# Moving the loads of an SSM's B and C, and the rows of B, between two DMA queues of a hybrid decoder block

## The chip, the cores and the metric

One core of a Trainium2 chip runs the whole block in one launch. The metric is the device time of that launch in microseconds (us), lower is better. The kernel before takes 1404.6 us (median of three runs, 1403.13 to 1407.8).

## What is computed

One residual block on x, 256 tokens by 2048 channels, in float32 (the batch and the depth are 1). Cut to what matters here:

```python
u = rms_norm(x, norm_mix_pre)
q, k, v, s_in, g_a, g_s = split(u @ w_in)          # 2048 x 8192
y_a = diff_attention(q, k, v, ...)                 # 8 heads, two softmax maps each
# S5: 64 groups of 16 channels, each drives one 64-state complex diagonal SSM
a_bar = exp(lam * dt)
b_bar = ((a_bar - 1) / lam)[..., None] * b         # (64, 64, 16), complex
bu = einsum('gph,lgh->lgp', b_bar, s_in)           # complex
states = scan(a_bar, bu)                           # over the 256 tokens
y_s = einsum('ghp,lgp->lgh', c, states).real + d * s_in
y_s = gelu(y_s); y_s = y_s * sigmoid(y_s @ w_glu + b_glu)
h = x + rms_norm((sigmoid(g_a)*(y_a@Wa) + sigmoid(g_s)*(y_s@Ws)) @ w_out)
out = h + rms_norm((silu(z@Wg) * (z@Wu)) @ Wd),  z = rms_norm(h)
```

## The kernel before, in words

**The main stream.** Nearly all of the time is a chain of dense products that TensorE does in blocks (`run_block`, line 254): one block is 256 tokens by 1024 columns, and goes through its rows of weights in steps k of 128. Each weight tile of 128x1024 (512 KB) is loaded by SyncE's queue into one of four buffers `raw` (line 186), then split in two: ScalarE rounds it (`hi`, line 205), VectorE subtracts (`lo`, line 206). Three products (hi by hi, lo by hi, hi by lo) of 512 columns for two token halves and two column halves are 12 matmuls for each k. `ensure` (line 210) keeps the splits up to two steps ahead and asks for loads up to four tiles beyond that. The first block makes the SSM's input, so it is called `ssm` and reads `w_in` from column 3072; then come q, k, v, the gates and so on.

**The start.** x is loaded in column pieces by SyncE's queue among the first weight tiles (`load_x0`, `load_x`, `first_load`, lines 340 to 347 and 972 to 980). TensorE transposes x piece by piece in the midst of the first block (`x_piece`, line 387; the tiles are `b` in the trace).

**Side tasks.** Everything else is Python generators that `pump` (line 230) advances after each step by a budget. `prep` (line 478) makes the SSM's constants: it loads the small parameters, B (`braw`, line 488) and C (`cn`, line 491) by GpSimd's queue; forms a_bar, sines and cosines on VectorE; multiplies B (`bb`); builds the rotation tables on GpSimd (lines 592 to 597); copies B's groups into block form (`blkB`, lines 617 and 618, ScalarE), transposes them, splits the result into `bh` and `bl` (tile `ga` in the trace), and writes it to DRAM as `stack_b` with twelve DMAs of 256 KB on SyncE's queue (line 627). `u_parts` (line 653) does the same for the SSM's input (`stack_u`, line 674). `ssm` (line 677) reads them back for each half group (`fetch`, line 706: `usf` and `bsf`, cast by ScalarE into `us` and `bs`), multiplies them (`bu_mm`), and rotates, scans and rotates back on VectorE, sixteen half groups in all. `table(hh)` (line 631, GpSimd) makes the rotation table of a half group's upper half, and `mirror` (line 649, ScalarE) fills the lower half from it.

**What sets the order.** Each engine and each queue works in one fixed order. The splits, matmuls and evacuations of the main stream are pinned to the order of the code (`InOrder`, line 31); side tasks on VectorE, ScalarE and TensorE, all of GpSimd's work and all DMA issues are not: a scheduler at build time places them by its own estimates of when each is ready, and among those that are ready takes the one that comes first in the code (line 1432). An instruction that has to wait on the chip holds up everything behind it on its engine or queue.

Of the kernel before, what the change touches and what calls it, by code (L numbers as in the profile page):

```python
# [88 lines left out]
def hybrid_block_kernel(  # L89
# [7 lines left out]
    nc = tc.nc  # L97
    pin = [True]
    V, A, T = (InOrder(tc, e, pin) for e in (nc.vector, nc.scalar, nc.tensor))
    G = nc.gpsimd  # L100
# [377 lines left out]
    def prep():  # L478
# [6 lines left out]
        braw = [big8(shape=(32, 2048)) for _ in range(2)]  # L485
        for ap, r, n in rows:
            G.dma_start(prow[r:r + n, :], ap)
        for t_, ap in zip(braw, (ssm_b_re, ssm_b_im)):
            G.dma_start(t_, ap[0].rearrange("(a g) p h -> a (g p h)", g=2))
        cn = [mixp.tile([P, NG, 64], F32, name=nm("cn")) for _ in range(2)]  # L490
        for t_, ap in zip(cn, (ssm_c_re, ssm_c_im)):
            G.dma_start(t_, ap[0].rearrange("(a g) h p -> (g h) a p", g=8))
        ldt = pp.tile([32, 2], F32, name="ldt")
        G.dma_start(ldt, ssm_log_dt[0].rearrange("(a g) -> a g", g=2))
        lamv = pp.tile([P, 4, 64], F32, name="lamv")
# [17 lines left out]
        e1 = pp.tile([P, 34], F32, name="e1")  # L513
        dve_exp(e1, e_in, 34, pp)
        yield 2.0

        nlam = const.tile([P, 1], F32, name="nlam")
        V.tensor_tensor(nlam, e1[:, 33:34], e1[:, 32:33], op=ALU.subtract)
# [8 lines left out]
        dve_exp(rr, adt, 32, pp)  # L527
        hold["rr"] = rr
        yield 2.0
        th = pp.tile([P, 8, 32], F32, name="th")  # L530
        V.tensor_tensor(th[:, 0, :], aim, dt, op=ALU.mult)
        for l in range(1, 8):
# [78 lines left out]
        for gg in range(NG // 2):  # L611
            ps = side()
            for e in range(2):
                g = 2 * gg + e
                for o in range(2):
                    t_ = blkB[e][o]
                    A.copy(t_[0:64, :, 0:16], bb[o][0:64, 4 * g:4 * g + 4, :])
                    A.copy(t_[64:128, :, 16:32], bb[o][64:128, 4 * g:4 * g + 4, :])
                    transpose(ps[:, (2 * e + o) * P:(2 * e + o + 1) * P], t_.rearrange("p a b -> p (a b)"))
            gs = slice(2 * gg, 2 * gg + 2)  # L620
            src = ps.rearrange("p (a o q) -> p a o q", a=2, o=2)
            A.copy(bh[:, gs].bitcast(F32R), src)
            V.tensor_tensor(bl[:, gs], src, bh[:, gs], op=ALU.subtract)
            yield 0.7
        for n, t_ in enumerate((bh, bh, bl)):
            for j in range(4):
                nc.sync.dma_start(stack_b[:, j // 2, n, :, j % 2].rearrange("g q o n -> q g o n"), t_[32 * j:32 * j + 32])  # L627
                yield 0.2


    def table(hh):
# [21 lines left out]
    def u_parts():  # L653

        un = hold["u"]
        uT = big8(shape=(P, 8, S))
        hold["yT"] = uT
        uh, ul = big8(shape=(P, 8, S)), big8(shape=(P, 8, S))
        for kk in range(4):
            ps = side()  # L660
            for j in range(2):
                for t in range(2):
                    k = 2 * kk + j
                    transpose(ps[:, j * S + t * P:j * S + t * P + P],
                              un[:, t * 1024 + k * P:t * 1024 + (k + 1) * P])
            ks = slice(2 * kk, 2 * kk + 2)
            fl = lambda t_: t_[:, ks, :].rearrange("p a b -> p (a b)")
            A.copy(fl(uT), ps)
            A.copy(fl(uh).bitcast(F32R), ps)
            V.tensor_tensor(fl(ul), ps, fl(uh), op=ALU.subtract)  # L670
            yield 0.6
        for n, t_ in enumerate((uh, ul, uh)):
            for j in range(4):
                nc.sync.dma_start(stack_u[:, j // 2, n, :, j % 2].rearrange("g q n -> q g n"), t_[32 * j:32 * j + 32])
                yield 0.3

    def ssm():
        uT = hold["yT"]
        nxt = table(0)
        mirror(*nxt)  # L680

        def finish(g, bC, sre, sim):
            yp = side()
# [44 lines left out]
        yield from group(0)  # L728
        fetch(0)
        bu = bu_mm(0)  # L730
        fetch(1)
        yield 1.0
        for hh in range(2 * NG):
# [703 lines left out]
```

## Time and profile before

| what | value |
|---|---|
| runs | 1407.8, 1403.13, 1404.6 us; median 1404.6 us |
| profiled execution | 1409.3 us, of which the span of the trace is 1407.5 us |
| TensorE (PE) | 1367.2 us busy, 97% of the span |
| VectorE (DVE) | 885.9 us, 63% |
| ScalarE (ACT) | 688.7 us, 49% |
| GpSimd (POOL) | 167.3 us, 12% |
| SyncE's DMA queue (q1) | 260.09 MB |
| GpSimd's DMA queue (q0) | 1.30 MB |

The span is the time from the first to the last recorded instruction; 1.8 us lie around it. Busy time of matmuls is modelled (they are pipelined), so the number of matmuls in a stretch and the clock that TensorE was granted tell more of its pace than its busy share. A row of the timeline gives start and length in us, engine, line, operation, destination and sources, and in brackets how long the engine sat idle before it and what ended that. L41 is the line of the helper that records all pinned engines' instructions, so there the tile's name tells what it is. SPq, ACTq and POOLq are the DMA issues of SyncE, ScalarE and GpSimd.

### The profile page before, as it was taken

The numbers are of one execution on the slowest core, as the hardware profiler recorded it, in microseconds if no ns is written. First come the engines' busy times: TensorE is split into PE (matmuls) and PEld (weight loads), VectorE is DVE, ScalarE is ACT, GpSimd is POOL, SyncE is SP. The second block draws the span as 40 slices with busy tenths as digits, with TensorE's granted clock in tenths as the row PEclk, the third lists the DMA queues.
The fourth block names the chain that finished last, engine by engine and source line by source line (L and its number), as shares of the span: only waits on it lengthen the run. The fifth ranks groups of instructions, "written<-read, shape, count | busy, mean of one in ns | idle before, by whom it ended". The sixth has DMA issues, their size and how long they took to land.

```text
span 1407.5 us, 17397 instructions
## 1 busy us (share of the span) xinstructions
PE 1367.2 (97%) x6367; PEld 1114.8 (79%) x6367; DVE 885.9 (63%) x1124; ACT 688.7 (49%) x1019; POOL 167.3 (12%) x187
## 2 busy tenths in 40 slices
PE   7999999999999989999999999999999999999997
PEld 6877777777777778888888888888888888888885
DVE  4954999768999957655754444444444445555555
ACT  3646545687544455444554434444444444444443
POOL 3090344202334100000000000000000000000001
PEclk8999999999999999999999999999999999999999
DMA  8678765454565657655765565655656555565551
GB/s 246 195 231 251 214 191 177 146 150 143 178 186 171 180 168 261 189 174 195 248 216 191 168 211 178 198 180 191 201 179 199 169 198 202 179 211 174 203 179 60
DMA packets 102006, 266.70 MB, mean 189 GB/s; under 512 B 10176, under 2 KB 17168, under 8 KB 98528
## 3 DMA queue, kind: packets, MB, share of 16 engines
q1 hardware_dynamic: 100704, 260.09, 57.6%
q10 hardware_dynamic: 608, 4.20, 0.8%
q0 software_dynamic: 608, 1.30, 0.4%
q8 instruction: 50, 0.82, 0.2%
q14 instruction: 36, 0.29, 0.1%
HBM read 257.16 MB, written 8.39 MB: 189 GB/s over the span
## 4 chain that ended last, share of the span: by engine, by line
issue 53%; PE 29%; DVE 9%; POOL 3%; ACT 3%; DMA 2%; SPq 1%; POOLq 0%; DVEq 0%; ACTq 0%
PE acc L41 26%; DVE lo L41 2%; PE side L41 2%; ACT hi L41 1%; DVE ssB L41 1%; DVE ssA L41 1%; DVE ssD L41 1%; DVE ssC L41 1%; DMA b<-in_x_dram 1%; SPq L627 1%; ACT b L41 1%; POOL tabS L644 1%; DVE ga L41 0%; DVE sim L41 0%; ACT prob L41 0%
## 5 line engine op out<-in xcount | busy, mean ns | idle before, releaser
L41 DVE TENSOR_TENSOR lo<-raw,hi 128x1024 fp32r<-128x1024 f32 (+1 forms) x341 | 422.6, 1242 | 256.2 <-ACT hi L41 246.5
L41 ACT CAST hi<-raw 128x1024 fp32r<-128x1024 f32 (+1 forms) x340 | 355.3, 1051 | 344.4 <-PE acc L41 278.8
L41 PE MATMUL acc<-lo,zT_h 128*128 128x512 f32 x704 | 275.1, 391 | 0.0
L41 PE MATMUL acc<-hi,zT_l 128*128 128x512 f32 x704 | 274.3, 390 | 0.0
L41 PE MATMUL acc<-hi,zT_h 128*128 128x512 f32 x704 | 271.2, 393 | 0.2 <-ACT zT_h L41 0.2
L41 DVE TENSOR_TENSOR lo<-b,hi 128x1024 fp32r<-128x1024 f32 x124 | 151.1, 1224 | 147.4 <-ACT hi L41 147.4
L41 PE MATMUL acc<-lo,xT_h 128*128 128x512 f32 x512 | 204.6, 403 | 2.6 <-DVE lo L41 2.4
L41 PE MATMUL acc<-hi,xT_l 128*128 128x512 f32 x512 | 202.0, 398 | 0.0
L41 ACT CAST hi<-b 128x1024 fp32r<-128x1024 f32 x124 | 130.6, 1053 | 120.4 <-PE acc L41 104.0
L41 PE MATMUL acc<-hi,xT_h 128*128 128x512 f32 x512 | 162.6, 403 | 5.2 <-ACT hi L41 3.1
L41 PEld LDWEIGHTS acc<-hi,zT_h 128*128 128x128 f32 x704 | 132.3, 188 | 27.6 <-ACT zT_h L41 0.7
L41 PEld LDWEIGHTS acc<-hi,zT_l 128*128 128x128 f32 x704 | 132.3, 188 | 27.6
L41 PEld LDWEIGHTS acc<-lo,zT_h 128*128 128x128 f32 x704 | 132.3, 188 | 26.5
L41 PEld LDWEIGHTS acc<-lo,xT_h 128*128 128x128 f32 x512 | 98.2, 192 | 27.4 <-DVE lo L41 4.9
L41 PEld LDWEIGHTS acc<-hi,xT_h 128*128 128x128 f32 x512 | 96.3, 191 | 27.9 <-ACT hi L41 5.6
L41 PEld LDWEIGHTS acc<-hi,xT_l 128*128 128x128 f32 x512 | 98.1, 192 | 19.8 <-issue 0.4
L41 PE MATMUL acc<-hi,b 128*128 128x512 f32 x256 | 82.9, 399 | 0.4 <-DVE b L41 0.3
L398 POOL TENSOR_TENSOR rstdf<-rstdfm,half 128x1 f32<-128x1 f32 x2 | 1.1, 546 | 691.6 <-DVE rstdfm L41 691.6
L41 PE MATMUL acc<-lo,hTh 128*128 128x512 f32 x176 | 68.6, 390 | 0.0
L41 PE MATMUL side<-hi,hTh 128*128 128x512 f32 x176 | 68.5, 389 | 0.0
L41 PE MATMUL side<-lo,hTh 128*128 128x512 f32 x176 | 68.5, 389 | 0.0
L41 PE MATMUL acc<-hi,hTh 128*128 128x512 f32 x176 | 68.4, 391 | 0.0
(213 smaller groups left out, 1699.2 us busy)
## 6 DMA issues: line engine op xcount, KB each, us to landing
raw<-in_w_in_dram SPq DMA_DIRECT2D x127, 512.0 KB, 4.1
raw<-in_w_ffn_gate_dram SPq DMA_DIRECT2D x96, 256.0 KB, 2.8
raw<-in_w_ffn_up_dram SPq DMA_DIRECT2D x96, 256.0 KB, 3.1
raw<-in_w_ffn_down_dram SPq DMA_DIRECT2D x44, 512.0 KB, 3.7
b<-in_w_ffn_down_dram SPq DMA_DIRECT2D x22, 1024.0 KB, 4.9
b<-in_w_ffn_gate_dram SPq DMA_DIRECT2D x40, 512.0 KB, 3.8
b<-in_w_ffn_up_dram SPq DMA_DIRECT2D x40, 512.0 KB, 4.7
raw<-in_w_out_dram SPq DMA_DIRECT2D x32, 512.0 KB, 4.4
```

Of the source, the lines that this page charges most:

```text
L41: ins = f(*a, **kw)
L398: G.tensor_tensor(r, ms, half[:, :n], op=ALU.pow)
L627: nc.sync.dma_start(stack_b[:, j // 2, n, :, j % 2].rearrange("g q o n -> q g o n"), t_[32 * j:32 * j + 32])
L644: G.tensor_tensor(up(tss), hi(sa), lo(cb), op=ALU.mult)
```

## The change

The bulk loads of B and C leave GpSimd's queue at the start of `prep` and go to SyncE's, B after the first exponential of `prep` and C after the second. Of each pair of copies into `blkB` the second goes from ScalarE to VectorE. The twelve writes of `stack_b` go from SyncE's queue to GpSimd's, with the six rows of first half groups ahead of the six of second half groups; those of `stack_u` take the same order and stay on SyncE's queue. The mirror of the first table stands after the first fetch and product in the code.

```diff
@@ prep
         braw = [big8(shape=(32, 2048)) for _ in range(2)]
         for ap, r, n in rows:
             G.dma_start(prow[r:r + n, :], ap)
-        for t_, ap in zip(braw, (ssm_b_re, ssm_b_im)):
-            G.dma_start(t_, ap[0].rearrange("(a g) p h -> a (g p h)", g=2))
         cn = [mixp.tile([P, NG, 64], F32, name=nm("cn")) for _ in range(2)]
-        for t_, ap in zip(cn, (ssm_c_re, ssm_c_im)):
-            G.dma_start(t_, ap[0].rearrange("(a g) h p -> (g h) a p", g=8))
...
         dve_exp(e1, e_in, 34, pp)
         yield 2.0
+        for t_, ap in zip(braw, (ssm_b_re, ssm_b_im)):
+            nc.sync.dma_start(t_, ap[0].rearrange("(a g) p h -> a (g p h)", g=2))
...
         dve_exp(rr, adt, 32, pp)
         hold["rr"] = rr
         yield 2.0
+        for t_, ap in zip(cn, (ssm_c_re, ssm_c_im)):
+            nc.sync.dma_start(t_, ap[0].rearrange("(a g) h p -> (g h) a p", g=8))
...
                     A.copy(t_[0:64, :, 0:16], bb[o][0:64, 4 * g:4 * g + 4, :])
-                    A.copy(t_[64:128, :, 16:32], bb[o][64:128, 4 * g:4 * g + 4, :])
+                    V.tensor_copy(t_[64:128, :, 16:32], bb[o][64:128, 4 * g:4 * g + 4, :])
...
-        for n, t_ in enumerate((bh, bh, bl)):
-            for j in range(4):
-                nc.sync.dma_start(stack_b[:, j // 2, n, :, j % 2].rearrange("g q o n -> q g o n"), t_[32 * j:32 * j + 32])
-                yield 0.2
+        for hf in range(2):
+            for n, t_ in enumerate((bh, bh, bl)):
+                for j in (2 * hf, 2 * hf + 1):
+                    G.dma_start(stack_b[:, hf, n, :, j % 2].rearrange("g q o n -> q g o n"), t_[32 * j:32 * j + 32])
+                yield 0.1
@@ u_parts
-        for n, t_ in enumerate((uh, ul, uh)):
-            for j in range(4):
-                nc.sync.dma_start(stack_u[:, j // 2, n, :, j % 2].rearrange("g q n -> q g n"), t_[32 * j:32 * j + 32])
-                yield 0.3
+        for hf in range(2):
+            for n, t_ in enumerate((uh, ul, uh)):
+                for j in (2 * hf, 2 * hf + 1):
+                    nc.sync.dma_start(stack_u[:, hf, n, :, j % 2].rearrange("g q n -> q g n"), t_[32 * j:32 * j + 32])
+                    yield 0.3
@@ ssm
         nxt = table(0)
-        mirror(*nxt)
...
         yield from group(0)
         fetch(0)
         bu = bu_mm(0)
+        mirror(*nxt)
         fetch(1)
```

## Rows read from the trace of the kernel before

**Rows 1.** The page: busy time, share of the span and instructions by engine.
```profile
PE 1367.2 (97%) x6367; PEld 1114.8 (79%) x6367; DVE 885.9 (63%) x1124; ACT 688.7 (49%) x1019; POOL 167.3 (12%) x187
```

**Rows 2.** Windows: length, busy us (and count) of PE, PEld, DVE, ACT, POOL, clock, DMA share, GB/s.
```profile
10.00:15.00 5.00, 0.47 (x1) 0.18 (x1) 1.62 (x2) 1.42 (x2) 1.46 (x3) 0.64 1.05 224
95.00:110.00 15.00, 12.62 (x49) 9.35 (x48) 5.00 (x5) 9.77 (x27) 10.28 (x16) 0.89 0.48 152
125.00:130.00 5.00, 5.00 (x24) 4.05 (x24) 1.23 (x1) 1.32 (x2) 0.00 (x0) 1.00 0.96 246
130.00:145.00 15.00, 12.27 (x48) 9.38 (x47) 6.64 (x8) 7.67 (x13) 0.00 (x0) 0.89 0.94 301
```

**Rows 3.** Timeline of the start: TensorE's two waits, GpSimd's late issue, SyncE's weight loads.
```profile
13.56 0.47 PE L41 MATMUL side<-ident,b 128*128 128x128 f32 x1 [4.13 <-DMA b<-in_x_dram]
14.59 0.53 POOL L497 DMA_DIRECT2D ga<-in_lambda_k_dram  x1 [3.48 <-DMA b<-in_ssm_b_re_dram]
...
16.76 0.90 PE L41 MATMUL side<-ident,b 128*128 128x128 f32 x3 [2.72 <-DMA b<-in_x_dram]
16.78 22.66 SPq L308 DMA_DIRECT2D raw<-in_w_in_dram  x8
```

**Rows 4.** DMA of 0 to 30 us: totals, queues, issues with KB each and us to landing.
```profile
DMA packets 3511, 8.10 MB, mean 270 GB/s; under 512 B 606, under 2 KB 1198, under 8 KB 3446
...
q0 software_dynamic: 608, 1.30, 18.4%
...
raw<-in_w_in_dram SPq DMA_DIRECT2D x8, 512.0 KB, 8.6
...
b<-in_ssm_b_re_dram POOLq DMA_DIRECT2D x1, 256.0 KB, 9.6
...
cn<-in_ssm_c_im_dram POOLq DMA_DIRECT2D x1, 256.0 KB, 12.7
```

**Rows 5.** Timeline, 66 to 105 us: GpSimd beside VectorE, then ScalarE and TensorE at the first table.
```profile
70.75 0.31 POOL L592 TENSOR_TENSOR sre<-tabc,ga 128x64 f32<-128x64 f32 x1
...
71.03 1.39 DVE L41 TENSOR_TENSOR lo<-raw,hi 128x1024 fp32r<-128x1024 f32 x1
...
71.41 1.22 POOL L594 TENSOR_TENSOR tabc<-sre 128x64 f32<-128x64 f32 x1
...
86.94 1.03 ACT L41 COPY blkB<-bb 64x64 f32<-64x64 f32 x4 [4.41 <-DVE bb L41]
...
99.81 0.40 ACT L41 COPY tabC<-tabC 128x256 f32<-128x256 f32 x1 [7.90 <-POOL tabC L643]
...
101.63 0.33 PE L41 MATMUL side<-ident,blkB 128*128 128x128 f32 x1 [2.17 <-ACT blkB L41]
...
104.63 0.41 ACT L41 COPY tabC<-tabC 128x256 f32<-128x256 f32 x1
```

**Rows 6.** Timeline, 117 to 155 us: SyncE's queue, then who waited, then GpSimd's next work.
```profile
117.64 11.99 SPq L627 DMA_DIRECT2D stack_b<-ga  x12
...
131.91 0.37 SPq L711 DMA_DIRECT2D bsf<-stack_b  x1
...
135.03 1.04 ACT L41 CAST hi<-raw 128x1024 fp32r<-128x1024 f32 x1 [8.70 <-DMA raw<-in_w_in_dram]
136.13 1.21 PE L41 MATMUL acc<-hi,xT_h 128*128 128x512 f32 x4 [2.68 <-ACT hi L41]
138.71 0.62 ACT L41 CAST bs<-bsf 96x512 fp32r<-96x512 f32 x1 [0.42 <-DMA bsf<-stack_b]
154.55 2.68 POOL L644 TENSOR_TENSOR tabS<-tabs,tabc 128x256 f32<-128x256 f32 x1 [48.64 <-DVE ssB L41]
```

**Rows 7.** The chain that ended last: start us, length us, what.
```profile
4.49 12.22 DMA b<-in_x_dram
...
129.73 5.21 DMA raw<-in_w_in_dram
```

**Rows 8.** DMA issues of the whole span: KB each and us to landing.
```profile
stack_b<-ga SPq DMA_DIRECT2D x12, 256.0 KB, 4.4
```

## The prediction, made before the changed kernel was run

> **What bounds the kernel now.** I read the page first: TensorE is busy for 97% of the span and no other engine for more than 63% [rows 1]. So the time is TensorE's work plus the stretches in which it falls behind, and a change that takes no matmul away can only win back such stretches. The view that finds them counts matmuls by window. An undisturbed window of 5 us has 24 at the full clock, 0.208 us each [rows 2]; three stretches in the reach of the diff have far fewer.
>
> The first is the start: one matmul from 10 to 15 us, at DMA engines that are full (share 1.05) [rows 2]. The timeline shows TensorE waiting for x twice, 4.13 and 2.72 us, until 16.76 us [rows 3], and the chain that ended last runs through that load of x for 12.22 us [rows 7]. Beside x and the weights, GpSimd's queue moves 1.30 MB and takes 18.4% of the DMA engines in the first 30 us; 1.05 MB of it are the four loads of B and C, which land 9.6 to 12.7 us after their issue [rows 4].
>
> The second is 95 to 110 us: 49 matmuls where 72 fit, so 23 x 0.208 = 4.8 us are lost [rows 2]. ScalarE stands 7.90 us before the mirror of the first table because GpSimd has not finished it, and TensorE's own wait of 2.17 us ends on ScalarE's copy into the block form of B [rows 5]. The rest of the loss is the clock: the mean granted over the window is 0.89 [rows 2], so part of it ran at the lower of TensorE's two levels, 1.2 instead of 2.4 GHz.
>
> The third is 130 to 145 us: 48 of 72, 24 x 0.208 = 5.0 us lost [rows 2]. SyncE's queue is occupied by the twelve writes of B's rows for 11.99 us, the weights come behind them, ScalarE waits 8.70 us for a tile and TensorE 2.68 us for ScalarE [rows 6]; the chain names that very load, 5.21 us [rows 7].
>
> **The change part by part.** The profiled execution took 1409.3 us, 4.7 above the median of the runs; each term below is taken off its time and the sum then carried to the median.
>
> *B and C off the start.* At the mean rate of the first 30 us, 270 GB/s, 1.05 MB take 3.9 us; by GpSimd's share of the engines (18.4% of 30 us, times 1.05/1.30) 4.5 us [rows 4]. The last of it landed after the wait for x had ended, so I take 3.5. The most that can be won is the whole wait, 4.13 + 2.72 = 6.9 us; the least is nothing, if the loads come so early on SyncE's queue that they delay the weight tiles that TensorE needs next. The four loads cost SyncE issue time: at 1.0 us each, as the writes of B's rows (11.99 / 12) [rows 6], 4 us. That is covered, since SyncE spreads eight weight issues over 22.66 us [rows 3]; without that cover the 4 us would count. GpSimd gets through its issues sooner too: the one at 14.59 us stood 3.48 us for the landing of B [rows 3]. Nobody needs it earlier.
>
> *Half of the copies into block form to VectorE.* A copy takes ScalarE 1.03 / 4 = 0.26 us [rows 5]; sixteen move, 4.1 us. Only those count that ScalarE does while it catches up after its 7.90 us: four of the copies that stand between the next splits, 1.0 us. Bounds: nothing, and the 4.1. On VectorE the copies are covered, for it is busy for 5.00 of the 15 us [rows 2]; were it full they would cost what they win.
>
> *The mirror later in the code.* I cost it at nothing. Its place in the code is not its place on ScalarE: the second table's mirror, which stands in the code after the first scans, came at 104.63 us, right behind the first's, since the scheduler took it as soon as it held it ready [rows 5]. So I expect the first to stay where GpSimd's lag is met. Bounds: 0 and the rest of the second loss, 4.8 - 1.0 = 3.8 us.
>
> *B's rows on GpSimd's queue.* SyncE gets 11.99 us back, and with them the 5.0 us lost by TensorE. GpSimd's engine can take the issues: it does nothing until 154.55 us, after an idle time of 48.64 us, and what stands behind them is only the third half group's table [rows 6]. At 0.53 us an issue [rows 3] six take 3.2 us; with a landing of 9.6 us [rows 4] the first half is there some 13 us after its rows are ready, where before the last write was issued after 11 and landed in 4.4 [rows 8]. So the readback starts no later. New is that weights and rows now share the DMA engines: at the start, beside GpSimd's queue, a weight tile landed in 8.6 us [rows 4], and four buffers at one step of 12 x 0.208 = 2.5 us each hold 10.0 us, of which the split takes 1.04 [rows 6] and some 1.39 [rows 5] and leaves 7.6. A landing of 8.6 misses that by 1.0 us, which I add. Bounds of this new wait: 0, and the whole 5.0 given back or more (the rival below).
>
> The rule against this part is in the Trainium skill's page "DMA: Bandwidth & Descriptors", section "Issuing engines are not separate DMA queues": transfers from all queues run on the same 16 engines and interleave, so another issuer only saves issue time, usually small beside the transfer. Here the issue is not small by the rows: 1.0 us each against 4.4 to land [rows 6, 8]. By the rule alone, the sum would be that of the second rival.
>
> *The order of the rows and of the input's rows* adds and removes no DMA: the same twelve writes each. The first readback needs six instead of twelve; it is counted above. What lies behind 145 us is not touched but may be scheduled in another order; I allow 2.2 us either way, the shortest of TensorE's waits on an engine above [rows 5].
>
> **Sum:** 3.5 + 1.0 + 5.0 - 1.0 = 8.5 us: 1409.3 becomes 1400.8, and the median 1404.6 becomes **1396.1**.
>
> **The rivals.** *The mirror does move* behind the splits, and ScalarE no longer stands for 7.90 us: 3.8 us more, **1392.3**. For it: the splits then come first in the code. Against it: the row at 104.63.
>
> *The DMA engines are the bound, not the queues.* From 125 to 145 us their share is 0.94 to 0.96 [rows 2]; the rows take the same time whoever issues them and the third loss stays. Likewise B and C may only be shifted to before the next weights, so half of the 3.5 comes back. Left: 1.75 + 1.0 = 2.75, **1401.9**. Against it: four buffers stand between a late tile and TensorE, and the weights are no longer behind all twelve writes.
>
> *A wait for GpSimd's writes takes the place* (slower). SyncE's read of the rows waits for their landing with weights behind it. GpSimd is stretched beside VectorE's subtractions: the same shape took 0.31 and, beside one of 1.39, 1.22 us [rows 5]. If every issue had to wait for one, it took 0.53 + 1.39 = 1.9 us: six 11.5, twelve 23. With 12.7 to land, the halves come 24 and 36 us after their rows are ready. If SyncE stands before both reads, from 11 us on, it is held up for about 24 us in all. The old hold of 12.0 cost 5.0, so 7.0 are covered; 24 cost 17, and less the 9.5 won elsewhere the time is 7.5 longer, **1412.1**. It decides from a hold of 7.0 + 9.5 + 4.2 = 20.7 us. Against it: the rows show no such stretch of an issue, and VectorE is busy for a quarter of 125 to 130 us [rows 2]. The Trainium skill's "SBUF — State Buffer", section "SBUF: two separate sides", speaks for it: while VectorE holds the shared port pair, GpSimd cannot write descriptors, and it advises the SP or ACT queue. The stretched row agrees for an arithmetic instruction; for a DMA issue no row here shows it.
>
> **How the numbers follow.** A measurement of this kernel can tell about 0.3%, 4.2 us, from no change. Chances: forecast 0.45, mirror moves 0.18, DMA engines bound 0.24, the new wait 0.13. The first two are faster, and a quarter of the third: 0.69. The rest of the third is within 0.3%: 0.18. The last is slower: 0.13. Range: the low end wins everything, 6.9 + 4.8 + 5.0 = 16.7, so 1387.9, rounded to 1388.0; the high end is the second rival with all of the start's gain given back, 1404.6 - 1.0 = 1403.6.
>
> **What would show it.** Right: TensorE's waits for x shrink to about half and end near 13 us; SyncE shows only weights and readbacks where the twelve writes were, and no split waits over 3 us for a tile there; the 7.90 us before the mirror stay. Wrong: a wait of the bs cast or of SyncE's read on the rows of 5 us or more; GpSimd's issues near 2 us; B's loads ahead of x; or a new stretch with under 20 matmuls behind 145 us.

## The result and the profile after

The changed kernel is slower: 1414.6 us median (1412.5 to 1417.2, five executions) against 1406.5 us (1403.1 to 1407.8, five executions) for the kernel before in the same series, a ratio of 1.0060 with a 95% interval of 1.0046 to 1.0074. That is about 8 us, nearly twice the 4.2 that the prediction held to be the least a measurement can tell from no change, and it lies above the forecast range. The profiled execution took 1414.5 us, its span is 1412.7. The trace of the kernel before has a span of 1407.5, from an execution of 1409.3 us that stood 2.8 us above the median just given; so the two traces side by side show 5.2 us of the 8.

The page after, which answers to [rows 1]:

```profile
PE 1369.8 (97%) x6367; PEld 1116.3 (79%) x6367; DVE 888.3 (63%) x1140; ACT 685.1 (48%) x1003; POOL 167.6 (12%) x195
...
q0 software_dynamic: 1312, 3.39, 0.9%
...
stack_b<-ga POOLq DMA_DIRECT2D x12, 256.0 KB, 9.9
```

The matmuls are the same 6367, sixteen copies have moved from ScalarE to VectorE, eight DMA issues more stand on GpSimd and its queue moves 3.39 MB in place of 1.30; a write of B's rows lands in 9.9 us, before in 4.4 [rows 8]. The sums by engine tell nothing of 8 us. The windows do. Columns as in [rows 2], the number behind the first x being matmuls:

```profile
10.00:15.00 5.00, 3.74 (x18) 2.77 (x18) 2.54 (x5) 2.53 (x5) 0.00 (x0) 1.00 1.00 264
25.00:30.00 5.00, 2.15 (x11) 1.35 (x10) 2.21 (x4) 3.18 (x6) 0.00 (x0) 1.00 0.98 328
30.00:35.00 5.00, 5.00 (x19) 4.03 (x18) 4.86 (x15) 2.99 (x5) 0.00 (x0) 0.66 0.70 207
95.00:110.00 15.00, 15.00 (x73) 12.09 (x72) 11.15 (x21) 10.83 (x27) 6.33 (x7) 1.00 0.81 252
130.00:145.00 15.00, 15.00 (x70) 12.41 (x70) 6.26 (x6) 8.01 (x12) 0.00 (x0) 1.00 0.98 340
...
260.00:300.00 40.00, 35.86 (x183) 28.03 (x181) 24.86 (x50) 31.45 (x75) 9.03 (x8) 0.91 0.43 131
480.00:560.00 80.00, 70.36 (x390) 59.93 (x389) 54.27 (x70) 41.11 (x60) 0.00 (x0) 0.91 0.58 191
```

All three stretches of [rows 2] were won: 18 matmuls for 1 in the first, 73 for 49, 70 for 48. A new hole has come at 25 to 35 us (30 matmuls, before 52), and two stretches that nobody had looked at have lost more than was won. The kernel before did 221 and 416 matmuls in them:

```profile
260.00:300.00 40.00, 38.82 (x221) 29.80 (x220) 26.06 (x50) 33.27 (x84) 6.29 (x7) 1.00 0.45 137
480.00:560.00 80.00, 74.21 (x416) 64.12 (x416) 52.12 (x64) 43.16 (x64) 0.00 (x0) 0.96 0.62 202
```

Summed window by window, the changed kernel was 37 matmuls ahead at 205 us (7.7 us at 0.208), 32 ahead at 260, 6 behind at 300 and 28 behind at 560 (5.8 us; the spans differ by 5.2). From 570 us to the end the difference stays within three matmuls, so the whole result is made before that.

**The start.** Timeline, both engines in order of time:

```profile
11.03 0.55 PE L41 MATMUL side<-ident,b 128*128 128x128 f32 x3 [0.43 <-DMA b<-in_x_dram]
11.56 1.62 SPq L513 DMA_DIRECT2D b<-in_ssm_b_re_dram  x1
16.59 0.39 SPq L529 DMA_DIRECT2D cn<-in_ssm_c_re_dram  x1
17.28 0.36 SPq L308 DMA_DIRECT2D raw<-in_w_in_dram  x1
17.90 0.38 SPq L529 DMA_DIRECT2D cn<-in_ssm_c_im_dram  x1
20.28 24.34 SPq L308 DMA_DIRECT2D raw<-in_w_in_dram  x10
28.29 1.18 PE L41 MATMUL acc<-hi,xT_h 128*128 128x512 f32 x4 [2.78 <-ACT hi L41]
```

The waits for x of 4.13 and 2.72 us [rows 3] are gone; x is there 5.7 us sooner. But the code's place of the four loads, behind two exponentials, was no place in time: they depend on nothing that is computed, and were issued from 11.56 us on, three of the four ahead of the weight tile of 17.28. TensorE then waits 2.78 us for ScalarE's split of a weight. Ahead of that split ScalarE had stood 1.21 us for the landing of C, for a copy of it, and then 0.77 us for the weight tile. The clock falls to 0.66 of full speed in the window behind.

**The rows of B.**

```profile
94.75 0.41 ACT L41 COPY tabC<-tabC 128x256 f32<-128x256 f32 x1 [6.19 <-POOL tabC L644]
118.41 5.35 POOL L628 DMA_DIRECT2D stack_b<-ga  x9 [16.61 <-ACT cdup L41]
125.45 1.24 POOL L628 DMA_DIRECT2D stack_b<-ga  x2 [1.70 <-DMA stack_b<-ga]
136.85 0.33 SPq L712 DMA_DIRECT2D bsf<-stack_b  x1
141.49 0.62 ACT L41 CAST bs<-bsf 96x512 fp32r<-96x512 f32 x1 [1.34 <-DMA bsf<-stack_b]
146.00 0.68 DVE L41 TENSOR_TENSOR ssA<-side,tabC 128x512 f32<-128x512 f32 x1
```

SyncE's own waits, 110 to 150 us (total, times, longest):

```profile
SPq L712 <- DMA stack_b<-ga: 3.1, 1, 3.1
```

SyncE's occupation of 11.99 us is gone, and with it the splits' wait of 8.70 [rows 6]. The price: the first readback is issued at 136.85 in place of 131.91, its cast runs at 141.49 in place of 138.71, and the SSM's first multiplication starts at 146.00 us (before 143.19). The readback had been expected to need six of the rows only. The sixth landed at 130.65, 12.2 us behind the first issue, but SyncE stood 3.1 us for the rows and issued the readback right behind the landing of the tenth, at 136.78; in two other executions of this order (a_mirror8 and a_late7) it also went out less than 0.1 us behind the tenth. So the order by halves in the code did not free the readback earlier. In the kernel before the tenth had landed at 130.60. So TensorE was brought forward and the SSM, which runs beside it on VectorE, was put back.

**The handover from the SSM to attention,** where the lead is lost, on the engines in turn:

```profile
261.58 2.69 POOL L645 TENSOR_TENSOR tabS<-tabs,tabc 128x256 f32<-128x256 f32 x1 [9.56 <-DVE ssB L41]
264.23 2.27 POOL L642 TENSOR_TENSOR tabC<-tabc,tabc 128x256 f32<-128x256 f32 x1
...
267.34 0.40 ACT L41 COPY tabC<-tabC 128x256 f32<-128x256 f32 x1 [1.29 <-POOL tabC L644]
268.84 0.42 ACT L41 ACTIVATE tabS<-tabS 128x256 f32<-128x256 f32 x1 [1.09 <-POOL tabS L647]
269.16 1.03 ACT L41 CAST hi<-raw 128x1024 fp32r<-128x1024 f32 x1
270.10 0.80 ACT L41 ACTIVATE prob<-prob,rs 128x128 f32<-128x128 f32 x2
270.80 1.82 ACT L41 ACTIVATE ga<-acc,rstdx 128x512 f32<-128x512 f32 x3
271.52 0.80 PE L41 MATMUL acc<-hi,xT_h 128*128 128x512 f32 x1 [4.14 <-ACT ga L41]
```

Read it from below. TensorE has finished a block and stands 4.14 us for the evacuation of its result (`ga`). That stands on ScalarE behind the two mirrors of an SSM table, these behind GpSimd's making of the table, and that behind VectorE's last use of the buffer. Between them stand one split and two steps of attention, which were ready; every wait in the row is the SSM's. TensorE, ahead of its old time, meets an SSM that is behind its own. Behind the stop the clock is at 0.50, and the windows from 265 to 280 hold 18, 9 and 24 matmuls.

In the kernel before, the same mirror had run long before the evacuation was due, and TensorE's longest wait between 260 and 300 us was 0.7 us:

```profile
262.09 0.40 ACT L41 COPY tabC<-tabC 128x256 f32<-128x256 f32 x1
273.25 0.69 ACT L41 ACTIVATE ga<-acc,rstdx 128x512 f32<-128x512 f32 x1
```

**The gate before glu,** where the rest goes:

```profile
499.33 0.41 PE L41 MATMUL side<-sre,blkC 128*32 128x256 f32 x2 [2.26 <-DVE sre L41]
501.67 1.07 PE L41 MATMUL side<-sim,blkC 128*32 128x256 f32 x4 [1.70 <-DVE sim L41]
504.69 0.41 ACT L41 ACTIVATE b<-b 128x256 f32<-128x256 f32 x1
505.11 1.28 ACT L41 ACT_TABLE_LOAD   x1
507.43 2.41 ACT L41 ACTIVATE b<-acc,rstdx 128x512 f32<-128x512 f32 x4
508.16 1.95 PE L41 MATMUL acc<-b,hi 128*128 128x256 f32 x4 [5.42 <-ACT b L41]
```

The SSM's last matmuls wait for VectorE, its last Gelu (504.69) for them, and the evacuation that frees the banks for glu (507.43) stands behind that Gelu and a table load. The SSM's last sum on VectorE starts at 500.94 us, before at 492.45. The kernel before has the same gate, 4.5 us earlier, but another row holds it there:

```profile
498.88 1.05 ACT L41 CAST hi<-raw 128x1024 fp32r<-128x1024 f32 x1 [3.97 <-DMA raw<-in_w_glu_dram]
499.83 0.41 ACT L41 ACTIVATE b<-b 128x256 f32<-128x256 f32 x1
503.64 0.80 PE L41 MATMUL acc<-b,hi 128*128 128x256 f32 x2 [5.52 <-ACT b L41]
```

VectorE had finished the input of that last Gelu by 497.29 us. The Gelu stood behind a split that waited 3.97 us for a tile of `w_glu`, and the table load and the evacuation behind the Gelu. So the gate is ScalarE's order; the SSM's last result is what holds it in the changed kernel, and a weight tile in the kernel before.

### The profile page after: what moved, and what is told of

The parts are those of the page before. It is cut to its first block, busy times and chain, and to the rows that moved or that the text cites. A ratio compares the mean times of both kernels' runs of the same rounds, so it can differ in the third digit from the quotient of the medians.

```text
span 1412.7 us, 17423 instructions
## 1 busy us (share of the span) xinstructions
PE 1369.8 (97%) x6367; PEld 1116.3 (79%) x6367; DVE 888.3 (63%) x1140; ACT 685.1 (48%) x1003; POOL 167.6 (12%) x195
## 3 DMA queue, kind: packets, MB, share of 16 engines
q0 software_dynamic: 1312, 3.39, 0.9%
## 4 chain that ended last, share of the span: by engine, by line
issue 54%; PE 28%; DVE 11%; POOL 3%; ACT 2%; DMA 2%; SPq 0%; POOLq 0%; DVEq 0%; ACTq 0%
PE acc L41 25%; DVE lo L41 3%; PE side L41 3%; DVE ssB L41 2%; DVE ssD L41 2%; DVE ssA L41 1%; DVE ssC L41 1%; POOL tabS L645 1%; ACT hi L41 1%; DMA b<-in_x_dram 1%; DMA raw<-in_w_in_dram 1%; DVE sim L41 1%; POOL tabC L644 0%; DVE sre L41 0%; POOL tabC L642 0%
```

## The experiments

Each was run in turns with the kernel before; ratios are against it, with 95% intervals. Counts are matmuls per stretch, from the windows of each profiled execution; kernels that are not in the table have their numbers in the text:

| kernel | ratio (95%) | 0-40 | 40-110 | 110-145 | 145-260 | 260-300 | 300-480 | 480-560 | SSM's last sum |
|---|---|---|---|---|---|---|---|---|---|
| before | 1 | 154 | 316 | 141 | 535 | 221 | 839 | 416 | 492.5 |
| changed | 1.0060 (1.0046-1.0074) | 160 | 326 | 162 | 530 | 183 | 843 | 390 | 500.9 |
| a_rows_sync | 1.0062 (1.0047-1.0077) | 147 | 324 | 127 | 523 | 212 | 855 | 410 | 497.3 |
| b_bc | 1.0078 (1.0061-1.0095) | 160 | 325 | 131 | 519 | 215 | 833 | 408 | 498.9 |
| b_rows_g | 1.0022 (1.0012-1.0031) | 170 | 323 | 159 | 529 | 219 | 825 | 406 | 489.8 |
| bc_held | 1.0043 (1.0030-1.0057) | 174 | 316 | 132 | 534 | 210 | 831 | 410 | 495.7 |
| a_bc_back | 1.0025 (1.0013-1.0037) | 165 | 322 | 161 | 534 | 212 | 823 | 410 | 491.8 |
| b_mpool | 1.0014 (1.0001-1.0027) | 165 | 332 | 138 | 522 | 212 | 848 | 413 | 492.0 |
| a_mpool | 1.0027 (1.0015-1.0038) | 159 | 330 | 161 | 522 | 217 | 834 | 410 | 492.0 |
| a_late7 | 1.0041 (1.0027-1.0055) | 154 | 324 | 160 | 523 | 179 | 850 | 416 | 506.2 |
| b_late7 | 0.9989 (0.9978-1.0000) | 161 | 322 | 133 | 537 | 223 | 835 | 432 | 492.5 |
| a_mirror8 | 1.0032 (1.0016-1.0048) | 152 | 326 | 160 | 535 | 209 | 834 | 394 | 497.9 |
| a_mirror8_late7 | 0.9993 (0.9983-1.0004) | 155 | 325 | 161 | 535 | 209 | 834 | 425 | 500.1 |

Names with a_ start from the changed kernel, names with b_ from the kernel before. Executions of the same order differ by some ten matmuls in the first stretch, by up to eight in the next two and by up to twelve in 145 to 260, so a row is read against its group, not alone. The row of the kernel before is from an execution 3 to 5 us above the medians of its runs in these series, so a kernel whose row is a little ahead of it can still be the slower one (b_rows_g). Behind 260 us many matmuls are attention's shorter ones (221 in 38.82 busy us before, 0.176 us each), so 0.208 us is there an upper figure. The sum of a row's differences times 0.208 us agrees with the spans within 1.5 us (changed: 28 fewer, 5.8 us, spans 5.2; a_mirror8_late7: 22 more, 4.6 us, spans 5.4).

### Which part carries the loss

**a_rows_sync**: the rows back on SyncE's queue, in the new order.

```diff
-                    G.dma_start(stack_b[:, hf, n, :, j % 2].rearrange("g q o n -> q g o n"), t_[32 * j:32 * j + 32])
+                    nc.sync.dma_start(stack_b[:, hf, n, :, j % 2].rearrange("g q o n -> q g o n"), t_[32 * j:32 * j + 32])
```

> Two theories for the 8 us that the change costs (1414.6 against 1406.5). Theory 1, the chain of side work: from the first half group of the SSM (VectorE at 143.2 us before, 146.0 after) to glu (first matmul at 503.6 and 508.2) VectorE is full and sets the pace; TensorE's lead at 145 us (about 46 matmuls, 9.6 us) is waited away, and the time follows the start of the SSM. Theory 2, the changeover: the lead is lost at 265 to 280 us by an unlucky order on ScalarE when attention begins, whatever the SSM's start was. This run puts the twelve writes of B's rows back on SyncE's queue, still by halves. Theory 1: the first six writes land sooner than by GpSimd, the SSM starts 3 to 10 us earlier than after, and the time falls by about as much, to 1405 to 1411, although the weights wait behind the writes again. Theory 2: the weights' stall of 5 us returns and nothing is won, 1413 to 1419.

1.0062, as the changed kernel. The old stall is back (127 matmuls in 110 to 145 us, before 141, changed 162) and yet the time is the same: 35 matmuls, 7.3 us, won or lost there do not show at the end. The stop at the handover is not there (212 matmuls, TensorE's longest wait 1.4 us), as TensorE comes to it without a lead; at the gate it waits 7.3 us for the evacuation, before 5.5.

**b_bc**: of the change, only the loads of B and C on SyncE's queue.

```diff
-            G.dma_start(t_, ap[0].rearrange("(a g) p h -> a (g p h)", g=2))
+            nc.sync.dma_start(t_, ap[0].rearrange("(a g) p h -> a (g p h)", g=2))
...
-            G.dma_start(t_, ap[0].rearrange("(a g) h p -> (g h) a p", g=8))
+            nc.sync.dma_start(t_, ap[0].rearrange("(a g) h p -> (g h) a p", g=8))
```

> Only the loads of B and C are moved to SyncE's queue, in the kernel before. Theory 1: the rows of B and the SSM's start are tied to GpSimd's tables and ScalarE, not to TensorE's lead, so the 1.7 us that TensorE keeps from the start don't reach the end: 1405 to 1409. A theory in which the front end counts gives 1403 to 1405.

1.0078: this part alone costs as much as the whole change or more; both expected ranges lie far below. It has no stop at the handover either (215 matmuls), and TensorE's wait for the evacuation at the gate is 7.2 us. The SSM starts 6.0 us later than before (143.19):

```profile
136.07 1.04 ACT L41 CAST hi<-raw 128x1024 fp32r<-128x1024 f32 x1 [7.50 <-DMA raw<-in_w_in_dram]
143.43 0.61 ACT L41 CAST bs<-bsf 96x512 fp32r<-96x512 f32 x1
149.19 0.69 DVE L41 TENSOR_TENSOR ssA<-side,tabC 128x512 f32<-128x512 f32 x1 [1.64 <-PE side L41]
```

The cast of B's first rows, at 143.43, waits for no transfer: it stands on ScalarE behind four splits, of which the first waited 7.50 us for its weight. It ran at 138.71 before [rows 6].

**b_rows_g**: only the rows on GpSimd's queue, in the new order.

```diff
...
-                nc.sync.dma_start(stack_b[:, j // 2, n, :, j % 2].rearrange("g q o n -> q g o n"), t_[32 * j:32 * j + 32])
...
+                    G.dma_start(stack_b[:, hf, n, :, j % 2].rearrange("g q o n -> q g o n"), t_[32 * j:32 * j + 32])
```

> Only the twelve writes of B's rows are moved to GpSimd's queue, by halves, in the kernel before. Theory 1: TensorE's stall of 5 us near 135 us goes, but the first readback comes no sooner, so the SSM starts where it did or some us later: 1406 to 1414. Theory 2 (this move is harmless, the loss is the changeover's): 1400 to 1404.

1.0022, 3 us slower, though 159 matmuls stand in 110 to 145 us. Those with the rows once on GpSimd's queue have 159 to 162 in this stretch, those with the rows on SyncE's 127 to 141 (a_nowait, whose SSM starts inside this stretch, has 150). The mechanism works in each of them; the time does not follow. Here the SSM is not late: it starts at 141.44 us, 1.8 us earlier than before, and TensorE has 41 matmuls more than before at 145 us. At the gate TensorE stands 8.00 us (before 5.52); the last sum was made at 489.82, but the last Gelu, at 497.25, stands behind a split that waited 2.10 us for a tile of `w_glu`. So a lead can also be given back there without a late SSM.

**a_nowait**: in the changed kernel the readbacks take rows of `w_in` in place of `stack_b`. It leaves out the use of B's rows.

```diff
-                nc.sync.dma_start(raw, st[g, hf].rearrange("s q j n -> (s q) j n" if tag == "us" else "s q j o n -> (s q) j (o n)"))
+                nc.sync.dma_start(raw, st[g, hf].rearrange("s q j n -> (s q) j n") if tag == "us" else w_in[96 * hh:96 * hh + 96, 0:512].rearrange("p (j n) -> p j n", j=2))
```

> The changed kernel with the sixteen readbacks of B's rows taken from rows of w_in instead (same shape and bytes; the rows of B are still written, but nothing reads them, so the SSM computes with other numbers): the SSM no longer waits for the rows. Theory 1: its first half group starts 20 to 40 us earlier, VectorE has more room before glu, and the time falls by 10 us or more, to below 1404. Theory 2: the start is not what costs; 1408 to 1416.

0.9952 (0.9938 to 0.9967), some 15 us under the changed kernel. The SSM starts at 109.07 us in place of 146.00 and its last sum at 469.98 in place of 500.94. When the SSM comes this early, the time comes down.

**bc_held**: b_bc with the loads of B held behind the first exponential and those of C behind the second, by a value written into the tile first.

```diff
+            V.tensor_copy(t_[:, 0:1], e1[0:32, 0:1])
             nc.sync.dma_start(t_, ap[0].rearrange("(a g) p h -> a (g p h)", g=2))
...
+            V.tensor_copy(t_[:, 0, 0:1], rr[:, 0:1])
             nc.sync.dma_start(t_, ap[0].rearrange("(a g) h p -> (g h) a p", g=8))
```

> As b_bc (only B and C move, 1414.7 us), but each load is held back until a value of the first or second exponential has been written into its tile, so it comes eight to fifteen weight tiles later in SyncE's queue. Theory A, the weights: in b_bc B and C stand ahead of the sixth weight tile and TensorE loses 21 matmuls at 30 to 40 us, which makes the whole preparation of the SSM later; held back, the lead of the start is kept, the SSM starts at 138 to 144 us instead of 149.2, and the time is 1399 to 1406. Theory B, late landing: what hurts is that B and C land later than they did from GpSimd's queue; held back they land later still, and the time is 1414 or more.

1.0043. Now the loads are issued at 34.66 and 48.83 us, and the first 40 us hold 174 matmuls, the most of any run (kernels with the loads early on SyncE: 147 to 160; on GpSimd: 154 to 170). But the SSM still starts at 147.90 us. Holding the loads back took 0.35% off b_bc's time and left 0.43%, between the two expected ranges: the weights of the first 40 us are a part of the loss, and the theory that they were its whole cause fell.

**a_bc_back**: the changed kernel with the four loads on GpSimd's queue again, at the start.

```diff
+        for t_, ap in zip(braw, (ssm_b_re, ssm_b_im)):
+            G.dma_start(t_, ap[0].rearrange("(a g) p h -> a (g p h)", g=2))
...
-            nc.sync.dma_start(t_, ap[0].rearrange("(a g) p h -> a (g p h)", g=2))
```

(and the same for C.)

> The changed kernel with the loads of B and C back on GpSimd's queue at the start, all else kept. If the move of B and C carries the loss (as it did alone), the SSM's first multiplication comes near 141 us and the time is 1404 to 1408, within 0.3% of the kernel before, though x again comes late at the start. Rival: the rows of B that land late by GpSimd's queue carry it; then the SSM still starts at 145 or later and the time stays at 1411 or above.

1.0025: 0.35% under the changed kernel, within the 0.3% expected. The SSM starts at 142.17 us. The last subtraction on B's rows runs at 113.72 us; in the changed kernel it runs at 118.99, behind the evacuation of the first block and two splits (b_bc has the same order, at 119.37), though the radii it goes back to (`rr`) were computed from 53.77 us on, against 57.92. The order of the instructions on VectorE and ScalarE is the scheduler's, and moving these loads changed it.

### Mirrors off ScalarE, and a late SSM without a loss

**b_mpool, a_mpool**: all mirrors on GpSimd.

```diff
-        A.copy(tcs[:, :, 0:P], tcs[:, :, S - 1:P - 1:-1])
-        A.mul(tss[:, :, 0:P], tss[:, :, S - 1:P - 1:-1], -1.0)
+        G.tensor_copy(tcs[:, :, 0:P], tcs[:, :, S - 1:P - 1:-1])
+        G.tensor_scalar(tss[:, :, 0:P], tss[:, :, S - 1:P - 1:-1], -1.0, None, op0=ALU.mult)
```

> The kernel before with the mirrors of all tables done by GpSimd right behind the tables, instead of by ScalarE. ScalarE no longer stands 7.90 us before the first mirror, with the copies into the block form of B behind it. Theory 1 (the time is the SSM's end plus some 925 us): the rows are ready 5 to 10 us earlier, the SSM starts at 134 to 139 us, and the time falls to 1395 to 1401. If instead the SSM's start didn't matter, only the stall of 4.8 us at 95 to 110 us would go and come back later: 1403 to 1407.

> The same in the changed kernel (1413 to 1415 us). Theory 1: the SSM's start moves from 146.0 to 137 to 141 us, 1404 to 1409. Otherwise 1412 to 1416.

In the kernel before it wins 14 to 27 matmuls by 110 us (against the two executions of the old order) and nothing at the end (1.0014, above both expected ranges). In the changed kernel it brings 1.0027, 0.33% under it. The time is that of theory 1, but not for its reason: the SSM's start does not move (145.61 us). The count says where the gain comes from: 217 matmuls from 260 to 300 us in place of 183.

**g_twice**: b_rows_g with the twelve rows written twice, so that the SSM starts late for certain.

```diff
-        for hf in range(2):
+        for hf in (0, 1, 0, 1):
             for n, t_ in enumerate((bh, bh, bl)):
```

> As b_rows_g (1408.2 us, SSM's start at 141.4), but GpSimd writes all twelve rows twice, first and second halves in turn, so the first readback has to wait for a second time round; SyncE's queue isn't held by them. Theory 1: the SSM starts 8 to 14 us later and the time is longer by about as much, 1415 to 1423. Theory 2 (the start isn't what costs): 1407 to 1411.

0.9996 (0.9985 to 1.0007), no loss and below both expected ranges, with an SSM that starts at 162.19 us and whose last sum comes at 504.01. In this build the scheduler had put the evacuation ahead of the last Gelu, and glu ran before the SSM had ended:

```profile
496.46 2.42 ACT L41 ACTIVATE b<-acc,rstdx 128x512 f32<-128x512 f32 x4 [0.30 <-PE acc L41]
497.62 0.66 PE L41 MATMUL acc<-b,hi 128*128 128x256 f32 x4
...
504.01 0.68 DVE L41 TENSOR_TENSOR sim<-ssB,ssD 128x512 f32<-128x512 f32 x1
```

So the SSM's lateness is not the loss itself. It costs where TensorE stands behind it.

### The two places, one at a time

**a_late7, b_late7**: the SSM's last result moved behind four of glu's eight steps.

```diff
-        finish(*pend)
         y1h, y1l = big8(F32R, (P, 8, S)), big8(F32R, (P, 8, S))
...
+        def last():
+            pin[0] = True
+            finish(*pend)
+            pin[0] = False
+            for _ in gelu((7,)):
+                pass
+        hold["last"] = last
+        yield from gelu(range(7))
...
-        before={6: lambda: cap(glu, 10, True)})
+        before={4: glu_last, 6: lambda: cap(glu, 10, True)})
```

(`gelu` holds the Gelus, the table's preload and the split of the parts named; `glu_last` calls `last` and then does what `glu_pre` did behind its `drain`.)

> The changed kernel with the SSM's last result (its matmuls, its Gelu, its split) moved behind the fourth of glu's eight steps; the other seven parts keep their place. My theory: the changed kernel has done as many matmuls as the one before at 500 us (5 fewer) and loses its time only in front of glu, where TensorE and ScalarE both stand behind the SSM's last result, which comes some 6 us later. Then the gap before glu closes and this run falls to 1398 to 1405, 8 to 15 us under the changed kernel, and within 2 us of the same edit made to the kernel before. Rival: the loss is made by waits of TensorE all along the SSM; then this stays 6 to 9 us above the same edit of the kernel before.

> The same edit made to the kernel before. My theory: its own gap before glu (x15, x6 and x26 matmuls in three slices of 5 us that hold 46 to 49 in a run without gap) closes as well, 1396 to 1402. Rival: about 6 to 9 us under the same edit of the changed kernel, as the pair without the edit.

The gate opens in both: 416 matmuls for 390 from 480 to 560 us, and 432 for 416. But each gains only 0.1 to 0.2%, about as much as the intervals leave open, and a_late7 stays 7 us above b_late7, as the rival had it. My theory that the gate was the whole fell here. The count from 260 to 300 us, 179, showed the larger place:

```profile
260.00:300.00 40.00, 35.86 (x179) 28.10 (x179) 25.10 (x45) 29.53 (x71) 8.34 (x7) 0.91 0.46 138
480.00:560.00 80.00, 74.59 (x416) 64.22 (x415) 58.86 (x76) 44.57 (x64) 0.00 (x0) 0.96 0.61 199
```

**rows_mirror_late7**: b_rows_g with all mirrors on GpSimd and the gate opened (the edits above together).

> The kernel before with B's rows on GpSimd's queue in the changed order, the mirrors on GpSimd, and the SSM's last result behind glu's fourth step: the parts that brought TensorE forward, with the gate moved. My theory: 1393 to 1399, under both kernels. Rival: the front's lead is lost along the SSM all the same, and it is no faster than the kernel before with the gate moved alone (within 2 us).

1.0000 (0.9989 to 1.0011). It has the best front of all (167, 334 and 160 matmuls in the first three stretches) and only 211 and 824 in 260 to 480 us. The expectation was missed by 5 us and more, and the rival came (b_late7 has 0.9989); a lead at 145 us is worth nothing by itself.

**a_mirror8**: the changed kernel, with the two mirrors of one table, the ninth, on GpSimd. The order of all else on ScalarE in front of the evacuation stays as it was.

```diff
-            if hh + 1 < 2 * NG:
+            if hh == 7:
+                tc_, ts_ = nxt
+                G.tensor_copy(tc_[:, :, 0:P], tc_[:, :, S - 1:P - 1:-1])
+                G.tensor_scalar(ts_[:, :, 0:P], ts_[:, :, S - 1:P - 1:-1], -1.0, None, op0=ALU.mult)
+            elif hh + 1 < 2 * NG:
                 mirror(*nxt)
```

> The changed kernel with the two mirrors of one table only (that of the SSM's ninth half group, made while the SSM hands over to attention) on GpSimd in place of ScalarE. If TensorE's stop at 267 to 271 us is made by these mirrors, which stand on ScalarE in front of the evacuation that TensorE waits for, the evacuation comes 2 to 3 us earlier, the stop of 4.1 us falls under 2, the loss of 38 matmuls between 260 and 300 us falls to 10 to 25, and the time falls by 3 to 5 us against the changed kernel: 1408 to 1410.5. Rival: the stop is only where a lead shows that the SSM's pace takes back in any case; then the time stays within 1.5 us of the changed kernel's 1413 and the gap before glu grows by what is won here.

1.0032: 0.28% or 3.9 us under the changed kernel, by two instructions of 0.40 and 0.42 us. TensorE's wait for the evacuation is 1.0 us in place of 4.1, the clock stays at 1.00, and the stretch holds 209. Windows of this run, then the longest of its three waits of TensorE from 260 to 300 us (total, times, longest; the others are 0.7 and 0.2):

```profile
260.00:300.00 40.00, 38.11 (x209) 29.34 (x208) 29.50 (x55) 30.94 (x75) 12.34 (x10) 1.00 0.49 141
270.00:275.00 5.00, 4.81 (x22) 3.91 (x23) 4.66 (x8) 4.97 (x8) 4.54 (x5) 1.00 0.56 172
480.00:560.00 80.00, 70.36 (x394) 59.86 (x393) 53.37 (x68) 39.79 (x60) 0.00 (x0) 0.91 0.57 191
```

```profile
PE acc L41 <- ACT ga L41: 1.0, 1, 1.0
```

The gate is still shut (394).

**a_mirror8_late7, a_mirrors_late7**: this edit, or all mirrors on GpSimd, with the gate opened too.

> The same with the SSM's last result behind glu's fourth step as well: both places of loss taken away. If they are the whole, the changed kernel comes out at 1402 to 1406, within 2 us of the kernel before with its gate moved (1402.4). Rival: 1407 or more, and a third loss is still to be found.

> The changed kernel with all mirrors on GpSimd and the gate moved. From the run with all mirrors (4.1 us over the kernel before) less what the moved gate gave the changed kernel (2 to 3 us): 1403 to 1406. If lower than 1402, the loads of B and C by SyncE's queue pay once the two places are gone.

0.9993 (0.9983 to 1.0004) and 0.9995 (0.9987 to 1.0004): no longer slower than the kernel before, and level with b_late7. With both places open, the changed kernel's loss of 0.6% is gone. Each place is worth more when the other is open: opening the gate takes 0.39% off a_mirror8, and moving the two mirrors takes 0.48% off a_late7, both clear of the intervals. The two mirrors were not moved in the kernel before with its gate open; its trace has no stop there that this could win. Windows of a_mirror8_late7:

```profile
260.00:300.00 40.00, 38.13 (x209) 29.35 (x208) 29.47 (x56) 31.04 (x76) 12.35 (x10) 1.00 0.50 145
480.00:560.00 80.00, 74.87 (x425) 63.94 (x424) 57.99 (x73) 47.44 (x69) 0.00 (x0) 0.98 0.66 220
```

**a_mirror8_late7_evac, b_late7_evac**: what takes back the rest of the lead (a_mirror8_late7 is 23 matmuls ahead of b_late7 at 260 us and 1 ahead at 560). VectorE is busy for the whole of most windows of the SSM; here the three evacuations of the q, k and v blocks that it makes go to ScalarE.

```diff
-        if eng[0] % 4:
+        if eng[0] % 4 or 4 < eng[0] <= 16:
```

> The changed kernel with the ninth table's mirrors on GpSimd, the SSM's last result behind glu's fourth step, and the three evacuations of the q, k and v blocks that VectorE made given to ScalarE (0.74 us each on VectorE, some 0.6 us each on ScalarE). If VectorE paces TensorE along the SSM: 1.5 to 2.5 us less than the run without this (0.9993 of the kernel before), so 0.9975 to 0.9985. Rival: VectorE is full but not the pace (ScalarE's order is); then no change or some loss, as the evacuations lengthen ScalarE's queue at the ends of the blocks.

> The same three evacuations moved in the kernel before with its gate moved (0.9989 of the kernel before): 0.997 to 0.998 if VectorE paces the SSM, 0.9985 to 1.0 if not.

0.9987 (0.9978 to 0.9996) and 0.9993 (0.9984 to 1.0002): 0.06% better in one, 0.04% worse in the other, both less than the intervals. This decides nothing; that VectorE's pace takes the rest is not shown. Apart from a_nowait, the first of the two is the one kernel whose interval lies under the kernel before, by 0.13%.

## Why the prediction was wrong, step by step

**B and C off the start: 3.5 us forecast, a small loss measured.** x did come early. The lower bound named the case that came: the loads come so early on SyncE's queue that they delay the weights. Over the groups above, the first 40 us hold 147 to 160 matmuls with the loads early on SyncE, 154 to 170 with them on GpSimd; held behind the weights, 174. The means are 154 (ten executions) and 163 (eight), so the move lost some 9 matmuls, 1.9 us, there. The rival that half of this is given back was nearer, and still too kind. What I had not asked is what the move does to the order behind it: b_bc and a_bc_back show this part alone putting the SSM back by 6.0 and 3.8 us and costing 0.78 and 0.35%.

**Copies into block form: 1.0 us forecast.** 40 to 110 us hold 324 to 326 matmuls in the changed kernel's order, 316 and 322 in that of before: a gain of 2 to 10 matmuls, 0.4 to 2.1 us. The size agrees; the copies' share was not measured by itself.

**The mirror: 0, right.** Moved in the code, it still came first on ScalarE, with 6.19 us of wait for GpSimd. Yet 95 to 110 us now hold 73 matmuls: GpSimd's table came 5 us earlier, and the weak stretch moved with it to 85 to 95 us (38 matmuls, before 47; clock 0.50 and 0.84 in its two halves).

**The rows: 5.0 us forecast, 5.0 measured** at 145 us (from 133 and 141 matmuls to 160, 160, 161 and 162: 24 x 0.208). In a_rows_sync, with the rows back on SyncE's queue, the stall is back. The Trainium skill's "DMA: Bandwidth & Descriptors", section "Issuing engines are not separate DMA queues", says that another issuer saves only issue time, usually small beside the transfer; in this stretch the issue time, 11.99 us of SyncE's queue, was not small, and freeing it was worth the whole of the stall.

**The new sharing wait: 1.0 us against, not seen by TensorE.** The landing took 9.9 us, in place of 4.4 before [rows 8] and near the 9.6 that the prediction took, and the weights did not suffer. The price fell on the SSM. "So the readback starts no later" was wrong: the first readback was issued 4.9 us later. The sixth row landed 12.2 us behind the first issue, as forecast (some 13), but the readback followed the tenth, 18.4 us behind it; in the kernel before, too, it had not waited for the twelfth (landed at 132.95, issue at 131.91). So "needs six instead of twelve" was wrong at both ends.

**What lies behind 145 us: "I allow 2.2 us either way". This is the step that failed.** By 145 us the forecast was sound: 28 matmuls ahead (the mean of four executions of the changed kernel's order less that of two of the old), 5.8 us of the 8.5. Behind it, 38 to 42 matmuls (7 to 9 us) went at the handover and 26 (5 us) at the gate. I had taken TensorE's lead for time won because TensorE is busy for 97% and "the time is TensorE's work plus the stretches in which it falls behind". From 145 us on the changed kernel's TensorE also stands, at two places, behind the SSM's chain on VectorE, GpSimd and ScalarE, and the change put that chain back: its first multiplication by 2.8 us, its last sum by 8.5 (in a_mirror8's execution by 4.5 and 5.4). a_mirror8 shows the handover by itself, and a_mirror8_late7 against a_mirror8 the gate; a_late7 alone gains no more than the intervals leave open. a_rows_sync and b_bc lose as much without the stop at the handover, so these two places are this kernel's and not the only way in which a late SSM costs.

**The rivals.** The one on the other side was 1412.1 us, near in time and wrong in place: it had SyncE held up between 110 and 145 us by the rows' landing, and this stretch is full (162). Its premise, rows that land late, a read and a cast that wait, is seen in small (3.1 and 1.34 us). The mirror that does move did not come; and with the DMA engines as the bound the third loss would have stayed, but 130 to 145 us hold 70 matmuls of 72 at a DMA share of 0.98, while of B and C even more than its half was given back. Of the signs that were to show the forecast wrong, the last came: "a new stretch with under 20 matmuls behind 145 us".

Left open: why the scheduler puts the last subtraction on B's rows behind the block's evacuation when B and C come by SyncE (only that it does is shown), why the first readback follows the tenth row, where a_rows_sync and b_bc lose the most, and what takes the rest of the lead.

## What to carry to other kernels

A lead of the busiest engine is worth what it still is at the next place where that engine stands behind another chain. Before a gain in an early stretch is added to the time, ask which side chain runs beside it, whether the change moves that chain the other way, and where the two meet next: look there for an evacuation that stands, on an engine that works in order, behind an instruction of the chain or behind one that waits for a weight. And a DMA's place in the code is no place in time: a load that depends on nothing goes out as early as the scheduler likes, so count it among what its queue carries at the start.

## What the runs showed of the hardware

A stop of TensorE costs more than its length. After the 4.14 us at the handover the clock was 0.50 over 270 to 275 us, 9 matmuls for 24; in a_mirror8, after stops of 1.0 us at most, it was 1.00 with 22. The edit took 3.1 us off the wait and brought 26 matmuls, 4.6 to 5.4 us at 0.176 to 0.208 each; the median time fell by 3.9 us.

GpSimd's issues were not stretched beside VectorE, against the premise of the rival: nine in 5.35 us, 0.59 each, with VectorE busy for 3.67 us of 118.4 to 123.8. But its tenth stood 1.70 us for the landing of an earlier one, which the twelve on SyncE had not shown. Its arithmetic was stretched: the product into `tabS` took 2.69 us at 261.58, while VectorE worked without a gap; a product of the same size at 267.39, with VectorE idle, took 0.62. The Trainium skill's "SBUF — State Buffer", section "SBUF: two separate sides", describes a port pair that the two engines hold in turn; this row agrees with it. By the rows of the handover the stretched product reached TensorE through the mirrors and the evacuation; no run tests this link by itself.
